# Input transposes moved in between the products of the first projection, with products of the identity ahead

## The chip, the cores and the metric

The kernel runs on one core of a Trainium2 chip. The metric is the device time of one execution in microseconds. A core has five engines, each with its own queue of instructions that it works through in order: TensorE (PE in the profile; its weight loads, PEld, overlap its products), VectorE (DVE), ScalarE (ACT), GpSimd (POOL) and SyncE (SP), which here does nothing but issue transfers. Transfers that an engine issues stand in that engine's queue like its other instructions; the data itself is moved by 16 DMA engines.

## What is computed

One layer of a decoder trunk on 256 tokens of 2048 channels, in float32:

```python
proj = x @ w_in[i]                                   # (256, 2048) @ (2048, 5136)
qkv_raw, z, b_raw, a_raw, u = jnp.split(proj, splits, axis=-1)
y_dn = gated_deltanet_group(qkv_raw, z, b_raw, a_raw, ...)   # conv, chunked delta rule, gated norm
y_pool = multiscale_pool_group(u, pool_w[i], pool_scale[i])
mix = jnp.concatenate([y_dn, y_pool], -1) @ w_out[i]
x = layer_norm(ALPHA * x + mix, ln1_g[i], ln1_b[i])
ffn = grouped_top2_moe(x, w_router, b_router, w_e_gate[i], w_e_up[i], w_e_down[i])   # 16 experts, width 1024
x = layer_norm(ALPHA * x + ffn, ln2_g[i], ln2_b[i])
x = x + jax.nn.sigmoid(x @ w_ple_gate[i]) * (p[i] @ w_ple_proj[i])
```

The change lies in the first line, the projection `x @ w_in`.

## The kernel before

All instructions are emitted in program order by hand (`tc.manual_schedule()`), so the order on each engine's queue is the order in which the Python code emits them. The projection runs over ten groups of 512 columns of w_in (line 597: q, k, v, z of the first four heads, and so on), each over the 16 blocks of 128 input channels, taken two at a time (`k0` = 0, 2, ..., 14; line 639). A two-block step is called a pair here.

A product needs x with its channels on the partitions, so x is turned by TensorE first. `xload(q)` (line 135) loads a quarter of x's channels, 512 of them, by two DMAs on SP. `xpose(k)` (line 142) turns the two blocks k and k+1 by four transposes into one PSUM tile; ACT casts it to `xh` (line 151, a rounded float32), and VectorE writes the rest, `xl`, as PSUM minus `xh` (line 152). The weights are split alike: `stream` (line 601) loads a piece of w_in (two blocks by 512 columns, 512 KB) by SP into one of four `raw` buffers, ACT casts each half to `hi` (line 610), VectorE subtracts to get `lo` (line 611); each `next(ws)` hands out one half. Every pair then makes 24 products (line 658): for each of four heads and two blocks, `hi` with `xh`, `hi` with `xl`, `lo` with `xh`, in this order. The first twelve go to PSUM bank 0 (`bk` = 0), the others to bank 1.

Ahead of the first group, `LOOK` = 3 times: a quarter of x is loaded, a pair is turned, a piece of w_in is loaded and split (lines 630 to 634). In the first group each pair first loads what is left of x, then turns the pair three ahead (`xpose(k0 + 2 * LOOK)`, lines 640 to 644), then splits half a piece for each bank (line 647), three pairs ahead of its use. So before the first product stand the turns of pairs 0, 2, 4 and 6, and those of pairs 8 to 14 follow one by one.

After each head's products, `step()` (line 524) advances the work in the background by one stage: evacuations, pooling, and the generators in `bg`. The first in `bg` is `gates()` (line 164). Its first stage, run at the first `step()` of the kernel, issues six small loads on ACT's queue (lines 171 to 176), among them one that spreads dt_bias over all partitions (line 175). It takes up x at a later stage, once all pairs are turned (`ready_k`, line 193). The psd pool has four PSUM tiles, which `xpose`, the gates and the delta rule share.

Of the kernel before, what the change touches and what calls it, by code (L numbers as in the profile page):

```python
# [26 lines left out]
KC = D // 128  # L27
LOOK = 3
# [15 lines left out]
def trunk(tc, x, p, w_in, conv_w, a_log, dt_bias, dn_norm_w, pool_w, pool_scale, w_out,  # L44
          ln1_g, ln1_b, w_router, b_router, w_e_gate, w_e_up, w_e_down, ln2_g, ln2_b,
          w_ple_proj, w_ple_gate, out):
    nc = tc.nc
    es = ExitStack()
    with es:
# [9 lines left out]
        ident = const.tile([128, 128], F32, name="ident")  # L59
# [69 lines left out]
        def psd(name):  # L129
            return pd.tile([128, 512], F32, name=name, tag="psd")  # L130
# [4 lines left out]
        def xload(q):  # L135
            for t in range(NB):
                nc.sync.dma_start(xs[t][q // 2].rearrange("p a b -> p (a b)")[:, q % 2 * 512:q % 2 * 512 + 512],
                                  x[t * 128:(t + 1) * 128, q * 512:(q + 1) * 512])
# [3 lines left out]
        def xpose(k):  # L142
            ready_k.extend((k, k + 1))
            ps = psd("xt")
            for j in range(2):
                for t in range(NB):
                    d = (k + j) % 8 * 128
                    nc.tensor.transpose(ps[:, j * 256 + t * 128:j * 256 + (t + 1) * 128],
                                        xs[t][k // 8].rearrange("p a b -> p (a b)")[:, d:d + 128], ident)
            dst = xh[:, k:k + 2].rearrange("p a b -> p (a b)")  # L150
            nc.scalar.copy(dst, ps)
            nc.vector.tensor_sub(xl[:, k:k + 2].rearrange("p a b -> p (a b)"), ps, dst)
# [371 lines left out]
        def step():  # L524
            for q in (evs, pools, bg):
                while q:
                    try:
                        next(q[0])
                        break
                    except StopIteration:  # L530
                        q.popleft()
# [61 lines left out]
        def evac(kind, hg, h0, ps):  # L593
            return zgate(hg, h0, ps) if kind == "z" else uin(hg, h0, ps) if kind == "u" else conv(kind, hg, h0, ps)
# [6 lines left out]
        def stream(srcs):  # L601

            for s in srcs:
                raws.rotate(1)
                raw = raws[0]()
                nc.sync.dma_start(raw, s.rearrange("(k p) c -> p k c", p=128))
                hi = hlH.tile([128, 2, 512], F32R, name="hi", tag="hl")
                lo = hlH.tile([128, 2, 512], F32R, name="lo", tag="hl")
                for k in range(2):
                    nc.scalar.copy(hi[:, k], raw[:, k])  # L610
                    nc.vector.tensor_sub(lo[:, k], raw[:, k], hi[:, k])  # L611
                    yield (hi, lo)

        def win_srcs():
            for kind, hg in order:
                c = base[kind] + 512 * hg
                for k in range(0, KC, 2):
                    yield w_in[k * 128:(k + 2) * 128, c:c + 512]

        def wout_srcs():  # L620
            for cs, ks in wout_order:
                for c in cs:
                    for k in ks:
                        yield w_out[k * 128:(k + 2) * 128, c * 512:(c + 1) * 512]
# [2 lines left out]
        wout_order = [((0, 1), (8, 10, 12, 14, 0, 2)), ((0, 1), (4, 6)), ((2,), range(0, KC, 2)), ((3,), range(0, KC, 2))]  # L627
        ws = stream(chain(win_srcs(), wout_srcs()))
        ready = deque()
        for n in range(LOOK):  # L630
            xload(n)
            xpose(2 * n)
            for _ in range(2):
                ready.append(next(ws))
        for gidx, (kind, hg) in enumerate(order):
            if kind == "q":
                bg.append(delta(hg, st[hg]))
            banks = [pp.tile([128, 2, 256], F32, name="pp", tag="pp") for _ in range(2)]
            for k0 in range(0, KC, 2):
                if gidx == 0:  # L640
                    if LOOK + k0 // 2 < 4:
                        xload(LOOK + k0 // 2)
                    if k0 + 2 * LOOK < KC:
                        xpose(k0 + 2 * LOOK)
                hi, lo = ready[0]
                for bk in range(2):
                    nxt = next(ws, None)
                    if nxt:
                        ready.append(nxt)
                    for h in (2 * bk, 2 * bk + 1):  # L650
                        hc = slice(h * 128, (h + 1) * 128)
                        o = banks[bk][:, h % 2]
                        for k in range(2):
                            kk = k0 + k
                            first = kk == 0 and h % 2 == 0
                            last = kk == KC - 1
                            for n, (a, b) in enumerate(((hi, xh), (hi, xl), (lo, xh))):
                                nc.tensor.matmul(o, a[:, k, hc], b[:, kk], start=(first and n == 0), stop=(last and n == 2),  # L658
                                                 skip_group_check=True)
                        if h % 2 and k0 == KC - 2:  # L660
                            evs.append(evac(kind, hg, h - 1, banks[bk]))
                        step()
                ready.popleft()
                ready.popleft()
            if gidx == 0:
                xs = None
# [57 lines left out]
        def pm():  # L724
            return pm_.tile([128, 512], F32, name="pm", tag="pm")
# [190 lines left out]
        ps = pm().rearrange("p (a e) -> p a e", e=NE)  # L916
# [74 lines left out]
        def pt():  # L991
            return psum.tile([128, 512], F32, name="pt", tag="pt")
# [274 lines left out]
        for c, (c0, w) in enumerate(CH):  # L1267
# [19 lines left out]
            for i in range(total):  # L1287
# [4 lines left out]
                n = 1024 // w * 128  # L1292
# [481 lines left out]
        warm = const.tile([128, 1], F32, name="warm")  # L1774
# [40 lines left out]
        ps = pt()  # L1815
# [4 lines left out]
        ps = None  # L1820
# [37 lines left out]
```

## Time and profile before

| | |
|---|---|
| time, median of 3 runs | 1529.66 us (1526.07, 1529.66, 1529.76) |
| time of the profiled execution | 1526.01 us |
| its span, first to last instruction | 1524.0 us |
| mean granted TensorE clock | 0.987 |
| TensorE busy | 1445.2 us (95%) |
| VectorE, ACT, POOL busy | 481.1, 320.6, 137.6 us |
| DMA, mean over the span | 321 GB/s, 489.61 MB |

The profile is of one execution, and times in it are microseconds from the start of its span. A line of a timeline tells when an instruction (or a run of equal ones, with their count) starts, how long it takes, its engine and source line, the tiles it writes and reads, and in brackets how long the engine sat idle before it and what ended that. An engine's name with a q (ACTq, SPq) stands for an instruction of its queue that issues a transfer. Records of products overlap, as products are pipelined: the pace is the distance of their starts. A float32 product of TensorE leaves two records, a transpose or a product of rounded operands one. The granted clock is 1.00 at 2.4 GHz and 0.50 at 1.2 GHz.

### The profile page before, as it was taken

What the parts mean: (1) busy time and instruction counts of PE and PEld (TensorE: products, weight loads), DVE (VectorE), ACT (ScalarE), POOL (GpSimd) and SP (SyncE); (2) the same over time, 40 slices, a digit from 0 to 9 for tenths busy, and PEclk for the clock granted to TensorE, in tenths of its full rate; (3) what the DMA queues carried; (4) which work ended last, traced back from release to release, by engine and by line L of the source; (5) the groups of instructions that cost most, each with busy time, mean ns of one, the idle gap of its engine ahead of it and who ended that gap; (6) DMA issues with size and microseconds to landing.
All of it is one profiled execution on the core that took longest, in us unless ns stands there. A gap on an engine that the chain in (4) does not pass through costs nothing.

```text
span 1524.0 us, 20057 instructions
## 1 busy us (share of the span) xinstructions
PE 1445.2 (95%) x8106; PEld 832.8 (55%) x8106; DVE 481.1 (32%) x924; ACT 320.6 (21%) x620; POOL 137.6 (9%) x218
## 2 busy tenths in 40 slices
PE   8999999999999999499999989898999999999997
PEld 8999998997873333133323333222333444447765
DVE  5886686765630102131101011010001001114335
ACT  5543453343430101010102020100000111002123
POOL 1251026411000000100000000000000000000032
PEclk9999999999999999699999999999999999999999
DMA  8553444445989999899999999999999999999991
GB/s 257 154 149 111 139 139 120 128 135 178 356 302 403 372 417 416 343 410 396 419 416 415 417 416 418 418 418 417 397 387 386 381 381 384 381 373 347 350 346 57
DMA packets 190706, 489.61 MB, mean 321 GB/s; under 512 B 16921, under 2 KB 63186, under 8 KB 168466
## 3 DMA queue, kind: packets, MB, share of 16 engines
q1 hardware_dynamic: 185680, 487.64, 85.8%
q8 instruction: 66, 1.08, 0.3%
q10 hardware_dynamic: 4850, 0.38, 0.3%
q14 instruction: 30, 0.25, 0.0%
q0 software_dynamic: 80, 0.26, 0.0%
HBM read 486.13 MB, written 2.10 MB: 320 GB/s over the span
## 4 chain that ended last, share of the span: by engine, by line
PE 38%; DMA 18%; DVE 1%; ACT 1%; POOL 0%; issue 0%; SPq 0%; ACTq 0%; POOLq 0%
PE pa L1115 13%; PE pa L1709 11%; DMA ring<-in_w_e_down 7%; PE pa L1627 4%; DMA ht<-in_w_e_gate 3%; DMA ht<-in_w_e_up 3%; PE pt L1034 2%; PE pt L1627 2%; DMA ring<-in_w_ple_proj 2%; PE pt L1525 2%; DMA pre<-in_w_e_gate 1%; DMA pre<-in_w_e_up 1%; PE pt L1446 1%; PE pt L1046 1%; DMA ht<-in_w_e_down 1%; DMA ht<-in_w_ple_gate 1%
## 5 line engine op out<-in xcount | busy, mean ns | idle before, releaser
L1115 PE MATMUL pa<-ring,X 128*64 128x512 f32 x768 | 185.8, 609 | 18.2 <-DMA pre<-in_w_e_up 6.6
L658 PE MATMUL pp<-xh,hi 128*128 128x256 f32 x640 | 188.3, 294 | 0.0
L658 PE MATMUL pp<-xl,hi 128*128 128x256 f32 x640 | 179.6, 281 | 0.0
L658 PE MATMUL pp<-xh,lo 128*128 128x256 f32 x640 | 179.4, 280 | 0.0
L611 DVE TENSOR_TENSOR lo<-raw,hi 128x512 fp32r<-128x512 f32 x206 | 148.6, 744 | 92.0 <-ACT hi L610 91.6
L1115 PE MATMUL pa<-ht,X 128*64 128x512 f32 x600 | 142.8, 601 | 9.1 <-DMA ht<-in_w_e_up 5.5
L610 ACT CAST hi<-raw 128x512 fp32r<-128x512 f32 x206 | 119.2, 618 | 142.5 <-PE pp L658 104.4
L1115 PE MATMUL pa<-pre,X 128*64 128x512 f32 x576 | 138.1, 601 | 2.1 <-DMA pre<-in_w_e_gate 1.5
L658 PEld LDWEIGHTS pp<-xh,hi 128*128 128x128 f32 x640 | 121.4, 190 | 0.2
L658 PEld LDWEIGHTS pp<-xl,hi 128*128 128x128 f32 x640 | 121.1, 189 | 0.1
L658 PEld LDWEIGHTS pp<-xh,lo 128*128 128x128 f32 x640 | 120.9, 189 | 0.0
L1115 PEld LDWEIGHTS pa<-ring,X 128*64 128x64 f32 x768 | 50.7, 138 | 119.7 <-issue 87.0
L1104 DVE SCALAR_TENSOR_TENSOR evac<-evac,pt 128x512 f32<-128x512 f32 x16 | 11.0, 686 | 254.9 <-ACT evac L1101 254.9
L1511 DVE SCALAR_TENSOR_TENSOR evac<-pa,gs,evac 128x512 fp32r<-128x512 f32 (+1 forms) x40 | 25.7, 641 | 189.5 <-ACT evac L1509 189.5
L1115 PEld LDWEIGHTS pa<-ht,X 128*64 128x64 f32 x600 | 38.5, 136 | 84.7 <-issue 61.9
L1115 PEld LDWEIGHTS pa<-pre,X 128*64 128x64 f32 x576 | 38.2, 137 | 79.5 <-issue 60.4
L1073 ACT COPY evac<-pa 128x512 f32<-128x512 f32 x32 | 18.8, 588 | 290.4 <-PE pa L1115 281.1
L1509 ACT ACTIVATE evac<-pa,gs 128x512 fp32r<-128x512 f32 (+1 forms) x40 | 24.0, 600 | 196.2 <-PE pa L1709 185.3
L1709 PE MATMUL pa<-ring,pre 128*64 128x512 f32 (+1 forms) x276 | 63.8, 507 | 1.2 <-DMA ring<-in_w_e_down 1.2
L1709 PE MATMUL pa<-ht,raw 128*64 128x512 f32 (+1 forms) x248 | 57.9, 522 | 1.8 <-DMA ht<-in_w_e_down 1.8
L1709 PE MATMUL pa<-ring,raw 128*64 128x512 f32 (+1 forms) x228 | 56.2, 517 | 0.8 <-DMA ring<-in_w_e_down 0.8
L1034 PE MATMUL pt<-x,P 128*64 128x512 f32 x224 | 52.9, 593 | 0.0
(386 smaller groups left out, 1898.9 us busy)
## 6 DMA issues: line engine op xcount, KB each, us to landing
ring<-in_w_e_gate SPq DMA_DIRECT2D x51, 1024.0 KB, 14.5
ring<-in_w_e_down SPq DMA_DIRECT2D x100, 512.0 KB, 10.8
ht<-in_w_e_down SPq DMA_DIRECT2D x95, 512.0 KB, 10.8
ring<-in_w_e_up SPq DMA_DIRECT2D x45, 1024.0 KB, 15.1
ht<-in_w_e_up SPq DMA_DIRECT2D x41, 1024.0 KB, 13.2
raw<-in_w_in SPq DMA_DIRECT2D x80, 512.0 KB, 3.7
pre<-in_w_e_up SPq DMA_DIRECT2D x74, 512.0 KB, 14.1
pre<-in_w_e_gate SPq DMA_DIRECT2D x70, 512.0 KB, 11.3
```

The costliest lines, as they stand in the source:

```text
L610: nc.scalar.copy(hi[:, k], raw[:, k])
L611: nc.vector.tensor_sub(lo[:, k], raw[:, k], hi[:, k])
L658: nc.tensor.matmul(o, a[:, k, hc], b[:, kk], start=(first and n == 0), stop=(last and n == 2), skip_group_check=True)
L1034: nc.tensor.matmul(ps[v], P[:, t, a], x1[:, t, c * 512:(c + 1) * 512], start=(t == 0), stop=(t == NB - 1))
L1046: nc.tensor.transpose(ps[:, i * 128:(i + 1) * 128], xg[c // 2][:, d:d + 128], ident)
L1073: nc.scalar.copy(raw, acc)
L1115: nc.tensor.matmul(acc[v], X(kk), w[:, h * 512:(h + 1) * 512], start=(kk == 0), stop=(kk == KC - 1))
L1509: nc.scalar.activation(yy[0], Y, AF.Copy, scale=gs[:, e:e + 1])
L1511: nc.vector.scalar_tensor_tensor(yy[1], Y, gs[:, e:e + 1], yy[0], op0=ALU.mult, op1=ALU.subtract)
L1525: nc.tensor.matmul(pR[c][t], C[:, e, t * 128:(t + 1) * 128], yy[n], start=(e == 0 and n == 0 and (t == 0 or w == 512)), stop=(e == NE // 2 ...
L1627: nc.tensor.matmul(ps[:, 0:S + 2], a[:, o:o + 128], b[:, k], start=(k == 0 and n == 0), stop=(k == kn - 1 and n == len(pairs) - 1))
L1709: nc.tensor.matmul(Y[v], HS[2 * e + a][:, f // 4, f % 4], two_[a][0][:, j * w:(j + 1) * w], start=(f == 0), stop=(f == 7))
```

## The change

Sixteen products of the identity with itself (128 x 128) are emitted first, into a PSUM tile of the psd pool that nobody reads. Of the turns ahead of the first group only that of pair 0 stays, after the first quarter of x. Each other pair is turned within the first group, one pair ahead of its use, ahead of the second bank's products and ahead of that bank's `next(ws)`; the loads of x stay where they are.

```diff
@@ -627,9 +627,15 @@
         wout_order = [((0, 1), (8, 10, 12, 14, 0, 2)), ((0, 1), (4, 6)), ((2,), range(0, KC, 2)), ((3,), range(0, KC, 2))]
         ws = stream(chain(win_srcs(), wout_srcs()))
         ready = deque()
+
+        ps = psd("warm")
+        for n in range(16):
+            nc.tensor.matmul(ps[:, 0:128], ident, ident, start=True, stop=True)
+        ps = None
         for n in range(LOOK):
             xload(n)
-            xpose(2 * n)
+            if n == 0:
+                xpose(0)
             for _ in range(2):
                 ready.append(next(ws))
         for gidx, (kind, hg) in enumerate(order):
@@ -640,10 +646,10 @@
                 if gidx == 0:
                     if LOOK + k0 // 2 < 4:
                         xload(LOOK + k0 // 2)
-                    if k0 + 2 * LOOK < KC:
-                        xpose(k0 + 2 * LOOK)
                 hi, lo = ready[0]
                 for bk in range(2):
+                    if gidx == 0 and bk and k0 + 2 < KC:
+                        xpose(k0 + 2)
                     nxt = next(ws, None)
                     if nxt:
                         ready.append(nxt)
```

## Rows read from the trace of the kernel before

**Rows 1.** Busy time by stretch: length, each engine's busy time (instructions), PEclk, DMA share, GB/s
```profile
36.00:440.00 404.00, 395.70 (x2934) 373.13 (x2931) 272.64 (x507) 157.82 (x312) 94.64 (x132) 1.00 0.52 164
...
780.00:1187.00 407.00, 376.49 (x1640) 125.77 (x1636) 42.49 (x86) 46.75 (x96) 3.01 (x14) 1.00 1.03 409
1187.00:1465.00 278.00, 277.00 (x1516) 157.09 (x1516) 60.08 (x105) 38.34 (x65) 3.41 (x6) 0.99 1.07 370
...
635.00:640.00 5.00, 2.53 (x8) 1.25 (x10) 1.34 (x2) 0.00 (x0) 3.19 (x6) 0.50 0.01 5
```

**Rows 2.** The chain of work that ended last, one piece of it: start, length
```profile
1163.52 10.82 DMA ring<-in_w_e_down
```

**Rows 3.** Timeline of TensorE, first group: start, length, operation, out<-in, idle before
```profile
8.39 1.76 PE L148 MATMUL xt<-ident,x 128*128 128x128 f32 x7 [0.18 <-DMA x<-in_x]
9.79 0.56 PE L658 MATMUL pp<-xh,hi 128*128 128x256 f32 x1
...
11.85 0.28 PE L658 MATMUL pp<-xh,hi 128*128 128x256 f32 x1
...
13.62 0.60 PE L148 MATMUL xt<-ident,x 128*128 128x128 f32 x4
13.98 0.37 PE L658 MATMUL pp<-xh,hi 128*128 128x256 f32 x1
14.18 0.28 PE L658 MATMUL pp<-xl,hi 128*128 128x256 f32 x1
14.30 0.28 PE L658 MATMUL pp<-xh,lo 128*128 128x256 f32 x1
...
35.29 0.28 PE L197 MATMUL ba<-xh,ba 128*32 128x256 f32 x1
```

**Rows 4.** Timeline of ACT and of its queue's transfers, the same stretch
```profile
6.35 0.58 ACT L151 CAST xh<-xt 128x512 fp32r<-128x512 f32 x1 [4.26 <-PE xt L148]
...
15.16 0.62 ACT L610 CAST hi<-raw 128x512 fp32r<-128x512 f32 x1 [1.07 <-DMA raw<-in_w_in]
15.17 0.38 ACTq L171 DMA_DIRECT2D rows<-in_conv_w  x1
...
16.91 2.21 ACTq L175 DMA_DIRECT2D dtb<-in_dt_bias  x1
19.16 0.44 ACTq L176 DMA_DIRECT2D alg<-in_a_log  x1
19.64 0.62 ACT L610 CAST hi<-raw 128x512 fp32r<-128x512 f32 x1 [3.85 <-DMA rows<-in_conv_w]
```

**Rows 5.** Timeline of VectorE, the same stretch
```profile
6.96 0.69 DVE L152 TENSOR_TENSOR xl<-xt,xh 128x512 fp32r<-128x512 f32 x1 [6.96 <-ACT xh L151]
...
20.29 0.69 DVE L611 TENSOR_TENSOR lo<-raw,hi 128x512 fp32r<-128x512 f32 x1 [3.79 <-ACT hi L610]
```

**Rows 6.** Busy time by short stretch around two restarts of TensorE
```profile
610.00:616.00 6.00, 0.08 (x2) 0.00 (x0) 0.18 (x1) 0.58 (x1) 0.00 (x0) 0.71 1.02 401
...
619.00:620.00 1.00, 1.00 (x6) 0.39 (x4) 0.00 (x0) 0.00 (x0) 0.00 (x0) 0.80 1.06 410
...
622.00:636.00 14.00, 0.00 (x0) 0.00 (x0) 0.00 (x0) 0.00 (x0) 0.00 (x0) 0.65 0.90 373
...
638.00:639.00 1.00, 1.00 (x5) 0.49 (x5) 0.37 (x1) 0.00 (x0) 1.00 (x2) 0.50 0.00 0
...
643.00:644.00 1.00, 1.00 (x8) 0.29 (x6) 0.00 (x0) 0.00 (x0) 0.00 (x0) 0.85 1.02 426
```

**Rows 7.** Timeline of POOL, where the identity is made
```profile
1.09 0.29 POOL L66 TENSOR_SCALAR_AFFINE_SELECT ident<-ones 128x128 f32<-128x128 f32 x1
```

**Rows 8.** Timeline of TensorE around four float32 products of the delta rule
```profile
176.57 1.05 PE L412 MATMUL pn<-bv,U 128*128 128x128 f32 x8
177.38 0.36 PE L658 MATMUL pp<-xh,hi 128*128 128x256 f32 x1
```

**Rows 9.** Waits of SP's queue, 36 to 440 us: total, times, longest
```profile
SPq L606 <- DVE lo L611: 192.9, 62, 8.6
```

## Prediction

> **What bounds the kernel now.** I read the busy time by stretches first. From 36 to 440 us (projections, delta rule, output product) TensorE is busy 395.7 of 404 us while the DMA engines stand at 0.52; from 780 to 1187 us the DMA share is 1.03 and TensorE is idle for 30.5 us; from 1187 to 1465 us both are full, TensorE at 277.0 of 278 [rows 1]. The chain of work that ended last says the same: loads of expert weights, 10.8 us each, one behind the other up to 1174 us, and products after that [rows 2]. So the head, where the change lies, goes at TensorE's pace, and only 8.3 us of its 404 are idle. The reader is to see in those rows that a delay of TensorE in the first 36 us has almost nothing to vanish into before 440 us. Whether it vanishes later is a rival below.
>
> Then I read the three queues of the first 36 us in order of time. TensorE starts its first product at 9.79 us, the second channel pair (k0=2) at 13.98 us, and ends group q0 at 35.29 us, where the gates' products follow, with one set of four transposes ahead of each of the pairs 2, 4, 6 and 8 [rows 3]. It never waits after 8.39 us. ACT is not so free. It waits for each piece of w_in to land: the fourth (for pair 6), whose first half is cast at 15.16 us, is waited for 1.07 us. Right behind that cast stand the six small loads that gates() issues on ACT's own queue, from 15.17 us to 19.16 + 0.44 = 19.60 us, one of them 2.21 us long, and the next cast runs only at 19.64 us [rows 4]. VectorE, which takes the low part, waits with it, until 20.29 us [rows 5]. Before the change this hold costs nothing, because xh of pairs 0 to 6 is made ahead of it.
>
> **The change part by part.** What ACT and VectorE do is the same in number; its place is not. Only xpose(0) stays ahead of the loop. xpose(2) is now emitted in the loop at k0=0, bk=1, that is after `next(ws)` of bk=0 (the cast of the fourth piece's first half) and after the first `step()`, which runs gates() to its first yield and so emits all six ACT loads. The schedule is by hand and the rows of ACT show exactly the order of emission. So the cast xh2 is moved on ACT past the casts of pieces 2, 3 and half of 4 and past the six issues; xl2 on VectorE past the same pieces' subtractions; the transposes on TensorE past twelve products. SP's queue keeps its order (xload and the w_in loads stand where they stood), POOL has nothing of it. Waiting behind xh2 are the second half of piece 4 on ACT, and on TensorE every product from k0=2 on.
>
> *The hold.* xh2 can start at 19.64 us, where ACT's next cast starts now. At 0.58 us [rows 4] it ends at 20.22; xl2 follows at once (xh0 started at 6.35 and its xl0 at 6.96, 0.03 us after the cast's end [rows 4, 5]) and takes 0.69 us, to 20.94. The second product of a pair reads xl, so it starts at about 20.97 us, against 14.18 us now [rows 3]: 6.8 us. This is a term on the path: TensorE has nothing else to do, since its queue is in order and delta() and the gates emit no product this early.
>
> *Transposes.* Now three sets (pairs 10, 12, 14) stand between 14.18 and 35.29 us; afterwards six (pairs 4 to 14). One set shifts the products by 13.98 - 13.62 = 0.36 us, and the first product after it takes 0.20 instead of 0.12 us, 0.44 us together [rows 3]. Three more are 1.3 us.
>
> *Clock.* TensorE is idle from about 12 us to 20.2 us and restarts slow. The rows show such restarts at the 1.2 GHz level (0.50 granted): after 6 us with 0.08 us of work, from 616 to about 619.4 us (0.80 in 619:620), at most 3.4 us; after 14 us without work, from 638 at the latest to about 643.3 us, 5.3 us [rows 6]. In the first stage the granted clock reads 1.00 throughout, but the pace tells: the nine products from 9.79 to 11.85 us stand 0.23 us apart on average, the fifteen from there to 13.62 us 0.118, so the engine was slow for 3.5 us from the transposes at 8.39 [rows 3]. Half speed for so long loses half of it: 1.7 to 2.6 us, or 1.4 if the wait for xl2 lies within the slow time. I take 1.7, from the row of the same stage.
>
> *Handovers of the later pairs.* Each pair now has its transposes only half a pair ahead. From their start to the second product of the next pair TensorE takes 0.36 + 0.20 + 11 x 0.118 + 0.12 = 1.98 us; transposes to their end 0.60, cast 0.58, subtraction 0.69 and two handovers of 0.03 make 1.93 us. That just fits, with hi of the piece three pairs on cast before it in bk=0. I take nothing. No row shows this chain without other work on ACT; if each handover were 0.15 us longer, six pairs would pay 0.3 us each, 1.8 us. A gain isn't possible here, as TensorE works without a wait now.
>
> *The sixteen products of the identity.* ident is ready at 1.09 + 0.29 = 1.38 us [rows 7]. Four f32 products of 128x128 leave eight records and take 177.38 - 176.57 = 0.81 us at full clock [rows 8]; sixteen take 3.2 us, or 6.5 at half, so they end between 4.6 and 7.9 us. The four transposes of pair 0, 0.8 us at half pace, then end at 8.7 us at the latest, and their cast, which starts at 6.35 us now [rows 4], slips by 2.4 us at worst. Their gain is that pair 0 may run at full pace (9 products x 0.11 = 1.0 us) and begin as much as 1.7 us before 9.79, as it no longer waits for x's second quarter. Neither gain nor loss counts: at half pace and begun only at 10.5 us, pair 0's 24 products and a set of transposes would still end by 10.5 + 24 x 0.213 + 0.8 = 16.4 us, 4 us before xh2. The cover is ACT's hold; without it these terms would be worth -2 to +2 us.
>
> *Sum.* 6.8 + 1.3 + 1.7 + 0 = 9.8 us, from 9.5 (short clock) to 12.5 (long clock, slow handovers). Against the profiled execution's 1526.0 us this is 1535.8 us. That execution stands at the lowest of the three runs, 3.6 us under their median of 1529.66, where the sum would be 1539.5 us. I put the forecast midway, at **1537.6 us**, as the runs don't say on which side a median of the changed kernel falls.
>
> **Rivals.** *A, not slower: the delay is given back by the transfers.* Place: the DMA-bound stretch from 780 to 1187 us. If its loads began as early as now, TensorE would only wait less there (it has 30.5 us of idle time [rows 1]), and the time would be 1526 to 1529.7 us. This decides if the first loads of expert weights don't move with TensorE. Against it: SP issues in order, and in the head its loads of w_in and w_out wait 62 times, 192.9 us in all, for the low parts that follow TensorE's use of the pieces [rows 9]; the expert weights queue behind them. The DMA engines even run dry between 635 and 640 us (share 0.01) [rows 1], so they are not one unbroken stream either.
>
> *B: the six issues are short.* Then xh2 follows the first half of piece 4 at 15.16 + 0.62 = 15.78 us, xl2 ends near 17.1, and the second product of pair 2 comes 2.9 us late: 2.9 + 1.3 + 1.7 = 5.9 us, 1531.9 to 1535.6 us. For it: 2.21 of the 4.43 us are one instruction, seen once [rows 4]. Against it: the other five alone are 2.2 us. The Trainium skill, page DMA: Bandwidth & Descriptors, section Issuing engines are not separate DMA queues, says that the time a sequencer takes to initiate a DMA is usually small relative to the DMA itself; by that rule ACT would hardly be held and this rival would be the result. The trace disagrees at this place, with 4.4 us of issue [rows 4].
>
> *C: slower handovers.* If every pair waits over 0.3 us for xl, the sum is 11.6 to 13 us: 1537.6 to 1542.7 us. Only the fit of 1.93 into 1.98 us speaks against it.
>
> **How the numbers follow.** Forecast 79, A 7, B 6, C 8 in 100. 9.5 to 12.5 us on the lowest run (1526.0) and on the median (1529.7) give 1535.5 to 1542.2; I reach down to 1533.5 to take in half of B, and stay at 1542 above. A measurement of this kernel can tell about 0.3%, 4.6 us, from no change. Slower by more: nearly all of the forecast and C, half of B, less a little for a low run of the changed kernel beside a high median of before, 0.84. Within it: A and the rest, 0.14. Faster: 0.02, since no row offers a gain that the hold doesn't swallow.
>
> **What would show it.** In the profile after: ACT's six issues unchanged near 15.2 to 19.6 us, then the cast of xh before the second half of the fourth piece; TensorE idle from about 12 to 20.2 us, released by ACT's xh, then products at half pace for some 3.5 us; the end of q0 near 45 us instead of 35.3; the same shift in SP's first loads of expert weights and in the stretch of full DMA. It would be wrong if xh2 is cast before the issues, if the idle time is gone, or if the shift at 45 us is no longer there at 780 us.

## The result, and the profile after

| | before | after |
|---|---|---|
| time, median of 6 runs each | 1526.55 us (1525.54 to 1529.76) | 1537.87 us (1534.89 to 1541.58) |
| ratio, 95% interval | | 1.0074 [1.0063, 1.0086] |
| profiled execution, its span | 1526.01, 1524.0 us | 1534.89, 1532.8 us |
| mean granted clock | 0.987 | 0.983 |
| first product of the gates (end of group q0) | 35.29 us | 45.64 us |
| TensorE's wait in q0 for a cast of x | none | 6.3 us, once |

The changed kernel is slower by 0.74%, 11.3 us between the medians; the forecast was 1537.6 us. The head of the trace is read first, queue by queue. ACT's queue and the transfers that it issues, after (columns as in [rows 4]):

```profile
12.32 1.15 ACT L610 CAST hi<-raw 128x512 fp32r<-128x512 f32 x2 [1.25 <-DMA raw<-in_w_in]
15.04 0.62 ACT L610 CAST hi<-raw 128x512 fp32r<-128x512 f32 x1 [1.57 <-DMA raw<-in_w_in]
15.04 0.38 ACTq L171 DMA_DIRECT2D rows<-in_conv_w  x1
...
16.77 2.30 ACTq L175 DMA_DIRECT2D dtb<-in_dt_bias  x1
19.12 0.44 ACTq L176 DMA_DIRECT2D alg<-in_a_log  x1
19.60 0.58 ACT L151 CAST xh<-xt 128x512 fp32r<-128x512 f32 x1 [3.94 <-DMA rows<-in_conv_w]
20.08 1.14 ACT L610 CAST hi<-raw 128x512 fp32r<-128x512 f32 x2
...
27.84 0.59 ACT L151 CAST xh<-xt 128x512 fp32r<-128x512 f32 x1 [1.49 <-PE xt L148]
```

The six issues stand where they stood, 15.04 to 19.56 us. What comes behind them at 19.60 us is now the cast of xh for pair 2, where before it was a cast of the fourth piece's second half. The bracket names the landing of `rows`, which this cast doesn't read; it starts 0.04 us behind the end of the last issue (19.12 + 0.44 us). VectorE's `xl` follows at 20.22 us. TensorE, after:

```profile
1.44 6.50 PE L633 MATMUL warm<-ident 128*128 128x128 f32 x32 [1.44 <-POOL ident L66]
...
9.56 0.39 PE L664 MATMUL pp<-xh,hi 128*128 128x256 f32 x1 [1.19 <-ACT hi L610]
...
11.91 0.60 PE L148 MATMUL xt<-ident,x 128*128 128x128 f32 x4
...
13.64 0.28 PE L664 MATMUL pp<-xh,lo 128*128 128x256 f32 x1
20.24 0.58 PE L664 MATMUL pp<-xh,hi 128*128 128x256 f32 x1 [6.31 <-ACT xh L151]
20.96 0.58 PE L664 MATMUL pp<-xl,hi 128*128 128x256 f32 x1
...
23.48 0.91 PE L148 MATMUL xt<-ident,x 128*128 128x128 f32 x4
24.15 0.37 PE L664 MATMUL pp<-xh,hi 128*128 128x256 f32 x1
...
27.20 0.60 PE L148 MATMUL xt<-ident,x 128*128 128x128 f32 x4
...
29.05 0.28 PE L664 MATMUL pp<-xh,hi 128*128 128x256 f32 x1
29.20 0.38 PE L664 MATMUL pp<-xl,hi 128*128 128x256 f32 x1
29.42 0.28 PE L664 MATMUL pp<-xh,lo 128*128 128x256 f32 x1
...
45.64 0.28 PE L197 MATMUL ba<-xh,ba 128*32 128x256 f32 x1
```

The reader is to see one hole, 6.31 us long up to 20.24 us, released by ACT's `xh`. The transposes that this cast reads had been done since 11.91 + 0.60 = 12.51 us. The second product of pair 2 starts at 20.96 us; in [rows 3] it is 14.18.

Busy time by stretch, after (columns as in [rows 1]); the first line lies in the hole, the second in the slow stretch behind it:

```profile
18.00:20.00 2.00, 0.00 (x0) 0.00 (x0) 0.00 (x0) 0.40 (x1) 0.00 (x0) 0.50 1.34 146
23.00:24.00 1.00, 1.00 (x7) 1.00 (x6) 0.00 (x0) 0.00 (x0) 0.00 (x0) 0.50 0.75 258
36.00:440.00 404.00, 396.72 (x2969) 376.40 (x2968) 275.56 (x509) 162.78 (x321) 94.76 (x132) 0.99 0.51 159
780.00:1187.00 407.00, 377.55 (x1648) 125.61 (x1650) 41.52 (x86) 44.51 (x91) 3.01 (x14) 1.00 1.03 410
1187.00:1465.00 278.00, 276.63 (x1478) 152.39 (x1474) 56.79 (x99) 38.60 (x67) 3.60 (x6) 0.99 1.07 371
```

The later stretches look as they did in [rows 1], only 10 us further on. The delay can be followed through the trace by events that both have: the end of q0 35.29 to 45.64 us (+10.35), the last product of the router (tile pL) 441.0 to 451.4 (+10.4), SP's first load of expert weights 378.7 to 388.8 (+10.1), and in the chain that ended last the load of [rows 2] from 1163.52 to

```profile
1172.26 10.81 DMA ring<-in_w_e_down
```

(+8.7). The span is longer by 8.8 us. The 1.5 us between +10.4 and +8.8 went at one place, the 48 transposes of line 1018 (now 1024). TensorE's timeline and the busy time there, before:

```profile
448.74 7.42 PE L1018 MATMUL pt<-P,x 128*128 128x128 f32 x48
```

```profile
450.00:452.00 2.00, 2.00 (x11) 2.00 (x11) 0.00 (x0) 0.00 (x0) 0.00 (x0) 0.50 1.01 426
```

The same two views after:

```profile
459.13 5.89 PE L1024 MATMUL pt<-P,x 128*128 128x128 f32 x48
```

```profile
460.40:462.40 2.00, 2.00 (x20) 2.00 (x19) 0.73 (x2) 0.26 (x1) 0.00 (x0) 1.00 1.01 426
```

The same instructions ran partly at the 1.2 GHz level in the profiled execution of before, and wholly at 2.4 GHz in that of after. Whether this belongs to the change was left to a second profile of the changed kernel (below).

### The profile page after: what moved, and what is told of

Its sections match the earlier page's. It is cut to its first block, busy times and chain, and to the rows that moved or that the text cites. A ratio compares the mean times of both kernels' runs of the same rounds, so it can differ in the third digit from the quotient of the medians.

```text
span 1532.8 us, 20121 instructions
## 1 busy us (share of the span) xinstructions
PE 1454.1 (95%) x8138; PEld 838.8 (55%) x8138; DVE 481.8 (31%) x924; ACT 321.6 (21%) x620; POOL 137.6 (9%) x218
## 4 chain that ended last, share of the span: by engine, by line
PE 36%; DMA 19%; DVE 1%; ACT 1%; POOL 0%; issue 0%; SPq 0%; POOLq 0%; DVEq 0%; ACTq 0%
PE pa L1121 12%; PE pa L1715 10%; DMA ring<-in_w_e_down 7%; PE pa L1633 4%; DMA ht<-in_w_e_up 4%; PE pt L1040 2%; PE pt L1633 2%; DMA ring<-in_w_e_gate 2%; DMA ring<-in_w_ple_proj 2%; PE pt L1531 2%; DMA ht<-in_w_ple_gate 1%; DMA ht<-in_w_e_gate 1%; DMA pre<-in_w_e_gate 1%; DMA pre<-in_w_e_up 1%; PE pt L1452 1%; DMA ht<-in_w_e_down 1%
## 6 DMA issues: line engine op xcount, KB each, us to landing
ring<-in_w_e_down SPq DMA_DIRECT2D x100, 512.0 KB, 10.7
ring<-in_w_e_up SPq DMA_DIRECT2D x45, 1024.0 KB, 16.2
```

## The experiments

The theory after the result: TensorE waits for the cast of pair 2, which was moved behind the weights up to the first half of piece 4 and behind ACT's six issues; everything else is a consequence (slow clock at the restart) or small. Rivals: the transposes in between cost by themselves; the identity products cost; a later stage gives the delay back.

**Two ways to take pair 2's cast out from behind the issues.** The first leaves the order alone and issues the six loads on SP:

```diff
-            nc.scalar.dma_start(rows[0:96, 0:128], conv_w...)
+            nc.sync.dma_start(rows[0:96, 0:128], conv_w...)
...
-            nc.scalar.dma_start(alg, a_log...)
+            nc.sync.dma_start(alg, a_log...)
```

> The changed kernel with the six small loads of gates() on SP's queue instead of ACT's. Hold theory (the changed kernel is late because the cast xh of pair 2 stands on ACT behind these six issues): ACT goes straight from the first half of piece 4 (cast at about 15.0 us) to xh2 at 15.6 us, the second product of pair 2 comes at about 17 us instead of 20.96, group q0 ends near 40.5 us instead of 45.64, and the whole is 4 to 6 us faster than the changed kernel, 1532 to 1534 us. It doesn't come back to the kernel before, as xh2 still waits for piece 4 to land. Rival (the time is the transposes' and the identity's own, or the late weights'): no change against the changed kernel, 1537 to 1539 us, q0 ending near 45 us.

Measured: 1534.75 us, ratio 1.0052 [1.0036, 1.0069], 3.1 us better than the change alone; q0 ends at 43.0 us. ACT:

```profile
15.76 0.62 ACT L610 CAST hi<-raw 128x512 fp32r<-128x512 f32 x1 [2.12 <-DMA raw<-in_w_in]
16.29 0.58 ACT L151 CAST xh<-xt 128x512 fp32r<-128x512 f32 x1
16.77 0.62 ACT L610 CAST hi<-raw 128x512 fp32r<-128x512 f32 x1
21.09 0.62 ACT L610 CAST hi<-raw 128x512 fp32r<-128x512 f32 x1 [3.71 <-DMA raw<-in_w_in]
```

The cast of xh follows the first half of piece 4 at once (16.29 us, not 19.60), and TensorE's wait for it shrinks from 6.3 to 3.7 us. So the issues do hold the cast, but they are only a part of the hold. Pair 2's second product comes at 17.76 us: of the 6.8 us by which it is late in the changed kernel, 3.2 go with the issues (20.96 to 17.76) and 3.6 stay (14.18 to 17.76), as the cast still stands behind the first half of piece 4, which must land first. The gain is smaller than expected for two reasons that the trace shows: the clock stayed at 0.50 for 5.7 us after the restart (16.92 to about 22.6 us) where the changed kernel had 3.9 (20.24 to about 24.1), and piece 4 was cast at 15.76 instead of 15.04 us. The issues now hold SP, too: its next load of w_in goes out at 15.69 us, and ACT waits 3.71 us for that piece. TensorE doesn't feel this; from 17.76 us to the end of q0 no product waits 0.2 us or more for an operand.

The second turns every pair at its predecessor's head, before both halves of the piece:

```diff
+                if gidx == 0 and k0 + 2 < KC:
+                    xpose(k0 + 2)
                 hi, lo = ready[0]
                 for bk in range(2):
-                    if gidx == 0 and bk and k0 + 2 < KC:
-                        xpose(k0 + 2)
                     nxt = next(ws, None)
```

> The changed kernel with the transposes of the next pair at the head of each pair, ahead of both halves of the weight piece, and gates() unchanged. Hold theory: xh2 is now ahead of the six issues, behind piece 3 (cast from 12.3 us), so pair 2's second product comes at about 15 us; but xh4 is behind the issues, is cast after the second half of piece 4 at about 20.2 us, and pair 4 waits until 21.5 us where it had products from 17.3 us before the change: q0 ends near 41 us, the whole 3 to 5 us faster than the changed kernel, 1533 to 1535 us. If it is only the short distance between transposes and use: no stall at pair 4, and q0 ends near 37 us, 1528 to 1530 us. If it is the transposes' and the identity's own time: no change, 1537 to 1539 us.

Measured: 1533.72 us, 1.0047 [1.0030, 1.0064]; q0 ends at 43.0 us. xh of pair 2 is cast at 14.08 us, ahead of the issues (15.76 to 20.59 us). Now pair 4's cast stands behind them, at 21.16 us, and its first product waits until 21.79 us. The waits of TensorE, 0 to 50 us (total, times, longest):

```profile
PE pp L664 <- ACT xh L151: 2.5, 2, 1.3
PE pp L664 <- DVE xl L152: 1.0, 2, 0.5
```

The large hole has become four small ones, two of them at pair 2, whose cast stands behind piece 3 (cast from 13.04 us), and two at pair 4. So the hold is not gone, it catches the next pair, which has a pair's products of cover ahead of it. Two stretches at a granted clock of 0.50 (16.2 to 19.6 and 23 to 26.4 us) take what else was hoped for: q0 was expected to end near 41 us.

**The identity products.** The changed kernel without them:

```diff
-        ps = psd("warm")
-        for n in range(16):
-            nc.tensor.matmul(ps[:, 0:128], ident, ident, start=True, stop=True)
-        ps = None
```

> The changed kernel without the sixteen products of the identity. Hold theory: xh of pair 0 comes 2 us earlier (6.4 instead of 8.4 us) and pair 0's products start earlier at half pace, but pair 2 starts at 20.2 us as before, so q0 ends at 45.6 +- 0.3 us and the time is that of the changed kernel, 1537 to 1539 us. If the identity's products cost time on the path: 2 us less. If their warm start is worth something: 1 us more.

Measured: 1538.5 us, 1.0077 [1.0061, 1.0094]. The first product comes at 7.58 us, xh of pair 2 at 19.96; q0 ends at 47.1 us, since the clock stayed at 0.50 up to about 27.1 us. The time is that of the changed kernel within the interval: the products cost nothing here and gain nothing, as ACT's hold covers both. The other half of the test puts them alone into the kernel before, with every transpose at its old place:

```diff
         ready = deque()
+        ps = psd("warm")
+        for n in range(16):
+            nc.tensor.matmul(ps[:, 0:128], ident, ident, start=True, stop=True)
+        ps = None
         for n in range(LOOK):
```

> The kernel before with only the sixteen products of the identity added ahead; the transposes stay where they were. Hold theory: the products run at half pace until 7.8 us as in the changed kernel, all four sets of transposes and the first product come after that at full pace, about 9.7 us, so pair 0 is about 1 us shorter; xh of pair 6 and the casts ahead of the issues are done by 15 us as before, and pair 6 waits for the second half of piece 4 at 20.3 us at the latest, where it starts at 20.5 us before. So q0 ends within 0.5 us of 35.3 us and the time is that of before, 1526 to 1528 us. Rival: the identity's products delay the start, 1 to 2 us slower.

Measured: 1527.13 us, 1.0006 [0.9997, 1.0015]: no effect that can be told, though an effect of 1 to 2 us isn't excluded either; q0 ends at 36.8 us, later than expected. In its profile the spreading of dt_bias took longer, and for once the kernel's old order feels the hold too. Its ACT queue, and TensorE behind it:

```profile
17.00 3.69 ACTq L175 DMA_DIRECT2D dtb<-in_dt_bias  x1
```

```profile
21.88 0.39 PE L662 MATMUL pp<-xh,hi 128*128 128x256 f32 x1 [1.10 <-ACT hi L610]
```

With the issues ending at 21.2 instead of 19.6 us, pair 6's half of the weights comes 1.1 us late. So the cover of the kernel before is just about as long as the hold.

**Length of the hold.** Two more spreading loads of dt_bias behind the six:

```diff
             nc.scalar.dma_start(alg, a_log...)
+            for n in range(2):
+                nc.scalar.dma_start(more[:, n], dt_bias[None, :].to_broadcast([128, NH]))
```

> The changed kernel with two further loads behind the six on ACT's queue, each again dt_bias spread over all partitions (2.3 us of issue each there), into tiles nobody reads. Hold theory: ACT is held 4.5 us longer, xh2 comes at 24.1 instead of 19.6 us, q0 ends near 50 us, and the whole is 4 to 5 us slower than the changed kernel, 1541.5 to 1543 us: each microsecond of hold costs one. Rival (hold is covered, time from elsewhere): no change. If an issue takes less when it is repeated, the shift is that of its length in the trace.

```profile
19.58 0.93 ACTq L179 DMA_DIRECT2D more<-in_dt_bias  x2
```

Measured: 1539.87 us, 1.0083 [1.0066, 1.0100]. The size was missed: the two took 0.93 us together, not 2.2 each as the one before them. xh of pair 2 came at 20.55 and q0 ended at 46.6 us, about 1 us later for 1 us more of issue. The rest of the time is not the hold: the products stand some 0.12 us apart instead of 0.118 up to 392 us, 2.5 us there. The new tile moves later tiles; whether that is the cause was not tested. The experiment fails as a doubling; it tells that the 2.2 us don't belong to a dt_bias load as such.

So the load ahead of it was repeated as well, the sixteen columns of w_in that go to `wba`, into a passing tile:

```diff
+            more = t256("more")
+            nc.scalar.dma_start(more[:, 0:256]..., w_in[:, 4096:4112]...)
+            nc.scalar.dma_start(more[:, 256:256 + NH], dt_bias...)
```

> The changed kernel with the load of w_in's 16 gate columns (wba) and the load of dt_bias behind it both issued a second time on ACT, into a tile nobody reads; no other tile moves. The first try, two more loads of dt_bias, was shorter than meant: they took 0.46 us each, so the 2.2 us of the first one seem to be a wait behind wba's many small rows. If so, the pair takes 0.4 + 2 us again, xh2 comes at 22.1 us instead of 19.6, q0 ends near 48 us, and the whole is 2 to 3 us slower than the changed kernel, 1540 to 1541 us. If the 2.2 us belong to the first spreading load alone, the pair takes 0.9 us and all is 1 us later.

```profile
19.64 0.45 ACTq L178 DMA_DIRECT2D more<-in_w_in  x1
20.13 2.24 ACTq L179 DMA_DIRECT2D more<-in_dt_bias  x1
22.41 0.58 ACT L151 CAST xh<-xt 128x512 fp32r<-128x512 f32 x1 [6.65 <-DMA alg<-in_a_log]
```

Now the 2.2 us are there a second time. TensorE's wait for xh grows from 6.3 to 10.2 us and q0 ends at 49.0 us, 3.4 later than in the changed kernel. Time 1538.92 us, 1.0078 [1.0063, 1.0094]; that is 13.0 us above the before measured with it, where the change alone has 11.3. Expected were 2 to 3 us more than the change. The dose is seen at the head; at the end 1.7 of the 3.4 us are left, and the other 1.7 lie within what the two medians can miss by.

Last, the load of `wba` moved behind the other five, beside the changed kernel once more, unaltered (the second expectation is for this one):

```diff
-            nc.scalar.dma_start(wba, w_in[:, 4096:4112]...)
             nc.scalar.dma_start(dtb, dt_bias...)
             nc.scalar.dma_start(alg, a_log...)
+            nc.scalar.dma_start(wba, w_in[:, 4096:4112]...)
```

> The changed kernel with the load of the gate columns (wba, many rows of 64 bytes) issued last of the six instead of fourth, so that dt_bias and a_log don't stand behind it. If the 2.2 us issue of dt_bias is a wait behind wba's rows, as e8_twice shows, dt_bias takes about 0.46 us, the six end near 17.6 us, xh2 is cast 1.8 us earlier than in the changed kernel (17.8 instead of 19.6 us), q0 ends near 44 us instead of 45.6 and the whole is 1.5 to 2 us faster than the changed kernel. If the queue must take wba's rows before ACT goes on in any case, nothing changes.

> The changed kernel once more, on the chip of e9_last and with a second profile. Expected: 1537 to 1539 us, xh2 at 19.6 us, q0 ending at 45 to 46 us as in the first profile. Open is the 1.5 us that the first profile got back near 450 us, where the kernel before ran slow and the changed one didn't: if that is a matter of the execution, this profile may show the slow stretch there too, and a span 1.5 us longer.

ACT's queue with `wba` last:

```profile
16.69 0.37 ACTq L174 DMA_DIRECT2D dtb<-in_dt_bias  x1
17.08 0.45 ACTq L175 DMA_DIRECT2D alg<-in_a_log  x1
17.58 0.44 ACTq L176 DMA_DIRECT2D wba<-in_w_in  x1
18.06 0.59 ACT L151 CAST xh<-xt 128x512 fp32r<-128x512 f32 x1 [2.05 <-issue]
```

With nothing behind `wba`, the six issues take 2.6 us instead of 4.4 and the cast comes at 18.06 us (the changed kernel's second profile: 19.74). q0 ends at 45.2 us, there at 46.0: of 1.7 us won 0.8 are left, because the clock came back 6.5 us after the restart (18.70 to about 25.2 us) where the second profile of the change has 4.6 (20.37 to about 24.9). Times: 1536.1 us (1.0070 [1.0049, 1.0091]) and 1537.32 us (1.0075 [1.0055, 1.0095]); 1.2 us is the expected direction, but no more than the intervals allow either way.

The second profile also answers the question of the 1.5 us. Its q0 ends 10.7 us late and its span is 12.0 us longer than before's. The 48 transposes took 5.89 us again, but the clock fell a little earlier (busy time by stretch):

```profile
450.50:452.00 1.50, 1.50 (x14) 1.50 (x13) 0.58 (x4) 0.13 (x2) 0.74 (x2) 0.87 0.90 265
452.00:454.00 2.00, 2.00 (x4) 0.97 (x5) 1.45 (x9) 1.98 (x4) 0.00 (x0) 0.50 0.95 336
```

These transposes end at 456.2 us before, 465.0 in the first profile after (+8.9) and 466.0 in the second (+9.8), so here the slow stretch gave back 0.9 of the 10.7 us, not 1.5. The rest of the way to 12.0 comes late: this profile has a slow stretch of some 3 us near 1493 us, where before has none; before's is near 1387 us. The first profile after has one near 389 us that before lacks. So such drops are something that one execution has in one place, another in another. The 1.5 us are no gain of the change, the spans can be off by as much either way, and the medians (+11.3 us both times) contain the drops at random.

**The hold without the change, and the change without the hold.** The six loads on SP in the kernel before, by the same edit as in the first experiment:

```diff
-            nc.scalar.dma_start(rows[0:96, 0:128], conv_w...)
+            nc.sync.dma_start(rows[0:96, 0:128], conv_w...)
...
```

> The kernel before with the six small loads on SP's queue. Hold theory: the hold of ACT is covered in the kernel before, so taking it away changes nothing, 1526 to 1528 us; the fifth piece lands late (near 21 us as in the changed kernel with this edit), but it is needed for pair 8 at 23.9 us only. Rival (the hold costs the kernel before something too): 1 to 3 us faster.

Measured: 1525.82 us, 0.9998 [0.9988, 1.0007]; q0 ends at 36.2 us, 0.9 later, as the products ran at half pace up to 13.5 us (11.85 before). Without the transposes behind them, the issues on ACT cost nothing, as the prediction had it for the kernel before.

And the transposes in between, but two pairs ahead and ahead of the split of the weights, with the six loads on SP and six steps later, and nine identity products:

```diff
+            for _ in range(6):
+                yield
+            nc.sync.dma_start(rows[0:96, 0:128], conv_w...)
...
+            if n == 0:
+                xpose(2)
...
                 for bk in range(2):
-                    if gidx == 0 and bk and k0 + 2 < KC:
-                        xpose(k0 + 2)
-                    nxt = next(ws, None)
+                    nxt = next(ws, None) if gidx or bk else None
...
+                    if gidx == 0 and bk == 0:
+                        if k0 + 4 < KC:
+                            xpose(k0 + 4)
+                        ready.append(next(ws))
```

> Both aims without the hold: pair 2 is turned right behind the first piece's casts, every later pair two pairs ahead of its use, in the middle of a pair and ahead of the next piece's casts; the six loads go to SP's queue six steps later; nine products of the identity instead of sixteen. Hold theory: no wait of TensorE after its first product but small ones, first product at 8.1 to 8.5 us instead of 9.79, three more sets of transposes in between the products (+1.3 us), pair 0 at full pace (-1 us): q0 ends at 33.5 to 35.5 us, 1525 to 1527 us, 0 to 2 us faster than before and 11 us faster than the changed kernel. Rival (the transposes in between cost by themselves): 5 us or more slower than before.

Measured: 1525.47 us, 0.9991 [0.9981, 1.0001]. The waits of TensorE up to 40 us, all of them:

```profile
PE warm L635 <- POOL ident L66: 1.4, 1, 1.4
PE pp L666 <- ACT hi L612: 1.1, 1, 1.1
PE pp L666 <- DVE lo L613: 0.2, 1, 0.2
```

There is no wait for `xh` left. One for `xl` is too short for this view: pair 4's second product starts 0.39 us behind its first, at 15.33 us, since its cast stood behind piece 3 until 13.77 us. The first product starts at 7.55 us, q0 ends at 34.2 us, 1.1 earlier than before. Six sets of transposes stand in between here too, so beyond the 1.3 us priced for three more of them they are not what made the change slow. The 1.1 us are below what the medians can tell.

All kernels together, by the end of q0 in the one profile and by the medians against those of before measured with them:

| kernel | q0 ends later by | median above before's |
|---|---|---|
| two pairs ahead, loads late on SP | -1.1 us | -0.5 us |
| before, loads on SP | 0.9 | -0.1 |
| before, with identity products | 1.5 | 1.2 |
| change, turns at the pair's head | 7.7 | 6.8 |
| change, loads on SP | 7.7 | 7.8 |
| change, `wba` last | 9.9 | 10.1 |
| change | 10.4 (second profile 10.7) | 11.3 (second time 11.3) |
| change, two more dt_bias | 11.3 | 12.9 |
| change without identity products | 11.8 | 11.5 |
| change, `wba` and dt_bias twice | 13.7 | 13.0 |

What TensorE loses up to the end of q0 comes out at the end about one to one, over a range of 15 us. A single profile's q0 also holds how long the clock stayed low in it: between the kernels with the large hole, 3.8 to 6.6 us, worth up to 1.4 us.

## Why the prediction was right, and where its terms were off

The forecast, 1537.6 us, lies 0.3 us under the measured median. That closeness is partly chance: the midway point between 1526.0 and 1529.7 us as a base was a choice, and in four measurements before's median was 1525.95 to 1526.97 us. By the base of 1526.0 the sum gave 1535.8, 2 us short; between the medians the change costs 11.3 us, where the sum had 9.8. The terms at the end of q0, where the clock drop near 450 us doesn't come in, are the better test:

| term | predicted | measured, profile after |
|---|---|---|
| hold (second product of pair 2) | 6.8 us | 20.96 - 14.18 = 6.78 |
| three more sets of transposes | 1.3 | 3 x (0.36 + 0.08) = 1.3; 27.20 to 27.56 is again 0.36 |
| clock, beyond the hold | 1.7 (1.4 to 2.6) | 1.5 |
| handovers of later pairs | 0 (0 to 1.8) | 0.7 |
| identity products | 0 | 0 |
| sum | 9.8 | 10.3; the shift is 10.35 |

*Hold.* Every step is in the trace: the cast at 19.60 us (19.64 predicted), `xl` at 20.22, the product at 20.96 (20.97). The runs with the loads on SP and with `wba` last show that the issues are a part of it, and the run with both loads twice that it grows with them. The part without them, 3.6 us in the run with the loads on SP, is the wait for piece 4; the prediction had it under rival B, at 2.9 us.

*Clock.* Eleven products from 20.96 to 23.48 us took 2.52 us; in [rows 3] the same from 14.18 take 11 x 0.118 = 1.30. The transposes to the next product took 0.67 (23.48 to 24.15) instead of 0.36. Together 1.5 us. That this lies so near the 1.7 is luck. The prediction read a slow stretch of 3.5 us out of [rows 3], from the transposes at 8.39 us on, but TensorE was slow there from its first transposes (before):

```profile
4.83 2.33 PE L148 MATMUL xt<-ident,x 128*128 128x128 f32 x8 [4.83 <-DMA x<-in_x]
7.73 0.48 PE L148 MATMUL xt<-ident,x 128*128 128x128 f32 x1 [0.57 <-DMA x<-in_x]
```

Eight transposes took 2.33 us, where four take 0.60 at full clock (13.62 us in [rows 3]). So that stretch lasted from 4.83 to 11.85 us, 7.0 us, and is no measure of a restart. The bound was too narrow as well: over the profiles with the large hole the slow stretch after the restart lasted 3.8, 3.9, 4.6, 5.5, 5.7, 6.5 and 6.6 us, four of them longer than the 5.3 us of [rows 6], which the prediction had as the upper end.

*Handovers.* This is the term that was mis-sized. The prediction let 1.93 us fit into 1.98 and took nothing. In the trace the chain takes 0.64 (27.20 to the cast at 27.84), 0.62 (to `xl` at 28.46), and 0.74 to the product at 29.20: 2.00 us, 0.02 too long. VectorE, after:

```profile
28.46 0.69 DVE L152 TENSOR_TENSOR xl<-xt,xh 128x512 fp32r<-128x512 f32 x1 [1.38 <-ACT xh L151]
```

The prediction counted two handovers, but there are three: the product starts 0.05 us behind the end of `xl` (28.46 + 0.69 us). In the hold term it did count that one. So small a miss still costs 0.13 us each time, because the product after the late one is late as well: 29.05, 29.20, 29.42, where undisturbed ones stand 0.118 apart. Five of the six pairs pay this, 0.7 us. Pair 8 doesn't, for in the changed kernel's profile the gates' product of line 180 (in pair 6 before, at 22.72 us) falls between its transposes and its use and makes that way 0.1 us longer:

```profile
31.75 0.26 PE L180 MATMUL cols<-ident,rows 105*128 105x105 f32 x1
...
32.58 0.28 PE L664 MATMUL pp<-xh,hi 128*128 128x256 f32 x1
32.70 0.30 PE L664 MATMUL pp<-xl,hi 128*128 128x256 f32 x1
```

So 0.1 us more of cover was enough. A fit with a margin of 0.05 us should have been priced as a wait. This is rival C with 0.13 in place of 0.3 us.

*Identity products.* They ended at 7.9 us, the late end of the range given, because the clock was low up to about 7 us: 32 records in 6.3 us, 0.20 us apart. Pair 0 began at 9.56 us (8.33 in the second profile) against 9.79. ACT's hold swallows it, as said.

*Rival A, given back by the transfers:* false. The transfers begin later with TensorE, SP's first load of expert weights by 10.1 us, as its queue waits for the low parts [rows 9]. The table of all kernels shows nothing given back.

*Rival B, short issues:* false for the change, where they took 4.5 us. The run with `wba` last shows what it would have been: 2.6 us of issue. The Trainium skill, page DMA: Bandwidth & Descriptors, section Issuing engines are not separate DMA queues, says that the time to initiate a DMA is usually small relative to the DMA itself. At 0.23 to 0.56 us each the traces agree for five of the six issues (`wba` was issued in 0.41 us and took 4.4 us to land in the profile after), and disagree for the one behind `wba`, with 2.21 to 3.69 us.

What stays open: why the clock comes back after 3.8 us in one execution and 6.6 in another, and whether it is the many small rows of `wba` (2048 of 64 bytes) or something else about it that holds the next issue. No run changed its row size. The landing of `wba` is not what the next issue waits for: in the profile after that was at 20.7 us (16.34 + 4.4), and the issue behind it had ended at 19.07 us.

## What to carry to other kernels

A step that is moved nearer to its use is moved, on every in-order queue, behind all that stands between its old and its new place, the transfers that this engine issues included: list that per queue, and read from the rows which of it waits or is long. If the step must move, let it pass those first, or keep enough products between producer and user (turned one pair ahead, five of six pairs were late, as the chain was 0.02 us too long; turned two pairs ahead, one was). And before an early delay is called harmless, look whether the next bound starts at a time of its own or is set off by the delayed engine; here it was set off, and 10 us at the start were 10 us at the end.

## What the hardware showed that was not expected

- The time of an issue on an engine's queue depends on the one before it: spreading dt_bias took 0.37 us ahead of the load of `wba`, 2.21 to 3.69 behind it, and 0.46 (half of 0.93) where another spreading load stood between.
- A product that is 0.03 us late costs another 0.10 us at the one after it, five times in the profile after.
- Two executions of the same kernel, the changed one, have stretches of some 3 us at a granted clock of 0.50 at different places (near 452 us in one, not in the other). Such a stretch was worth 1.5 us at the 48 transposes of before, and about 0.4 us near 389 us in the profile after.
